# Norms of q taken per head behind its convolution, and exponentials of the broadcast gate rows loaded from DRAM

## The chip, the cores and the metric

The kernel runs on one core of a Trainium2 chip. A core has a matrix engine (TensorE, PE in the profile, with its weight loads as PEld), three engines for element-wise work (VectorE or DVE, ScalarE or ACT, GpSimd or POOL), and SyncE (SP), which here only issues DMAs. Each engine takes its instructions in program order and waits where an operand is not there yet; ACT issues DMAs too, in its own order. The metric is the device time of one execution in microseconds (us), lower is better.

## The reference, cut to what matters

One transformer-like layer works on 1024 latent tokens and 256 context tokens of width 1024. After a modulated norm, one projection feeds two mixers, a gated DeltaNet (four heads of 128, q, k and v through a short convolution) and a rotary retention; then come a gated output projection and a SwiGLU. The change touches the DeltaNet:

```python
y = short_conv(...)                       # 5 taps, then silu; q, k, v per head
q = l2_normalize(q) * (HEAD_DIM ** -0.5)
k = l2_normalize(k)
G = jnp.cumsum(gc, axis=-1)               # running log-decay in a chunk
diff = G[..., :, None] - G[..., None, :]
decay = where(incl, exp(diff), 0)
A = where(strict, (k beta) k^T * decay, 0)
u, w = solve(I + A, [v beta, k beta exp(G)])
qk = (q k^T) * decay
q_dec = q * exp(G)
```

Everything is float32. The kernel takes the norms out of the products: it keeps the sums of squares of q and k and applies them as scales later.

## The kernel before

The token axis is cut into `TT` = 10 tiles of 128 tokens: tiles 0 and 1 are the context, 2 to 9 the latents. There are 4 heads and two directions `d`. A float32 product is made of three passes over high and low parts (`hhi`, `hlo`, `whi`, `wlo`), so most groups of matmuls come as three lines (611 to 613, 371 to 373).

The stages that matter, in the order of the source: the gates (`G`, the cumulative log-decay, is transposed to rows and stored in the DRAM scratch `grow_d`); the convolutions of k (`conv_block(4 + h)`, then `kstat`, which transposes each k tile and takes its squared norm on ACT into `nk`); the convolutions of q (`conv_block(h)`, after which ACT's queue stores the head into the DRAM scratch `qd`, line 682); the two gate groups of the retention, `token_major` 6 and 7 (a `Silu` on ACT at line 532 evacuates their `tm` banks); then the solves. For each token tile `pre(t)` builds what the solve needs; for each of three batches of tiles (`BATCH`) `invert` computes the inverses of 32x32 diagonal blocks in 31 pairs of VectorE instructions (`tmp` at line 765, `X` at 767) and sends them through DRAM (`xd`), and `merge` puts the blocks together with small matmuls. The convolutions of v (`conv_block(8 + h)`, transposes `vT` at line 856, evacuation `vt` on ACT at 859) and the z groups 8 and 9 lie between them as matmul work.

`pre(t)`, lines 701 to 737: load `kc` (line 664); 4 matmuls `kk`; for the latent tiles (t >= 2) load `qc`, transpose it, square it with a row sum into `nq` (lines 710, 712), and 4 matmuls `kq`. Then for each direction: `gw` is loaded from `grow_d`, the same row broadcast to all 128 partitions (256 KB); POOL writes `e` from `gw` with the triangle filled (722); ACT takes 4 exponentials with a bias (726); VectorE multiplies `kk` by `e` into `ut` (730) and `kq` by `e` into `sp` (732); `ut` is stored (733). For t >= 2 ACT also takes the exponential of `gw` itself (735), POOL multiplies it by `qc` (736), and `sp` is stored (737). The pools give two buffers each to `kc`, `qc`, `gw`, `e`, `sp` and `ut`, and three PSUM banks to each of two groups, two to the convolutions.

The order of instructions on each engine is not that of the source: a scheduler with a simulated timeline places them when the program is built, so an edit in one place can move work in another.

Of the kernel before, what the change touches and what calls it, by code (L numbers as in the profile page):

```python
# [8 lines left out]
F32 = mybir.dt.float32  # L9
F32R = mybir.dt.float32r  # L10
I32 = mybir.dt.int32
AF = mybir.ActivationFunctionType
ALU = mybir.AluOpType
# [4 lines left out]
P = 128  # L18
D = 1024
KT = D // P  # L20
NCTX = 256
NLAT = 1024
NTOK = NCTX + NLAT
TT = NTOK // P
LT = NLAT // P
H = 4
# [4 lines left out]
FAR = -1e30  # L31
# [7 lines left out]
def build(nc, tc, ap, dbg=None, stop=None, marks=None):  # L39
    root = ExitStack()  # L40
    V, S, G, T, SY = nc.vector, nc.scalar, nc.gpsimd, nc.tensor, nc.sync
# [17 lines left out]
    def close(p):  # L59
        p_close.pop(id(p)).close()  # L60
# [16 lines left out]
    dr = pool("scratch", space=DRAM)  # L77
# [15 lines left out]
    def bank_b(name):  # L93
        return bank("pb", name)
# [96 lines left out]
    try:  # L191

        cc = const("cc", [P, KT, 2])
        ident = const("ident", [P, P])
# [37 lines left out]
        W2 = None  # L232
# [156 lines left out]
        def token_major(g, tiles, finish, store, pl, q=S):  # L389

            w = [tm_weights(g, kh, pl, q) for kh in range(2)]

            for p in range(0, len(tiles), 2):
                pair = [(t, tm_bank(g)) for t in tiles[p:p + 2]]
                for kh in range(2):
                    for t, o in pair:
                        tm_half(o, w[kh], kh, t)
                for t, o in pair:
                    tm_store(g, t, o, finish, store, pl)
# [47 lines left out]
        W2 = pool("w2", bufs=2)  # L447
# [97 lines left out]
        cw = GS.tile([P, 12, 5], F32, tag="cw", name="cw")  # L545
        SY.dma_start(cw, ap["cw"])
        grow_d = dr.tile([TT * 8, P], F32, tag="grow_d", name="grow_d")


        sd = dr.tile([TT, P, 10, 512], F32, tag="sd", name="sd")  # L550
# [4 lines left out]
        def c8(t, d):  # L555
            return slice(t * 8 + d * 4, t * 8 + d * 4 + 4)
# [39 lines left out]
        gT = AB.tile([80, P], F32, tag="gT", name="gT")  # L596
        V.tensor_copy(gT, ps[:80, :P])
        SY.dma_start(grow_d, gT)
        close(AB)
        CV = pool("cv", side="right")  # L600

# [72 lines left out]
        sv = rsqrt(GS, nkf, TT * H, "sv")  # L674
        V.tensor_tensor(sv, sv, nkf, ALU.mult)
        sv3 = sv.rearrange("p (t h) -> p t h", h=H)
        for h in range(H):
            y = newy()
            conv_block(h, y, True)
            if h < 2:  # L680
                ada_rest(5, h)
            S.dma_start(qd[:, :, h, :].rearrange("t p j -> p t j"),
                        y[:, NCTX:].rearrange("p (t j) -> p t j", j=P))

        checkpoint("q")
        for g in (6, 7):
            token_major(g, LAT, fin_gate, S, W2, SY)
        checkpoint("rg")
        close(R2)
        close(W2)  # L690
# [9 lines left out]
        def pre(t):  # L700
            b, c = where[t]
            kc = load(GP, kd[t], "kc", 2)
            pk = bank_b("kk")
            for h in range(H):
                T.matmul(pk[:, h * P:(h + 1) * P], kc[:, h, :], kc[:, h, :], start=True, stop=True)
            if t >= 2:
                qc = load(GP, qd[t - 2], "qc", 2)
                pn = bank_b("qt")
                for h in range(H):
                    T.transpose(pn[:, h * P:(h + 1) * P], qc[:, h, :], ident)  # L710
                for h in range(H):
                    S.activation(pn[:, h * P:(h + 1) * P], pn[:, h * P:(h + 1) * P], AF.Square, accum_out=nq[:, t - 2, h:h + 1])
                pq = bank_b("kq")
                for h in range(H):
                    T.matmul(pq[:, h * P:(h + 1) * P], kc[:, h, :], qc[:, h, :], start=True, stop=True)
            for d in range(2):
                gw = GP.tile([P, H, P], F32, tag="gw", name="gw", bufs=2)
                SY.dma_start(gw.rearrange("p h i -> p (h i)"),
                             grow_d[c8(t, d), :].rearrange("a b -> (a b)").partition_broadcast(P))
                e = GP.tile([P, H, P], F32, tag="e", name="e", bufs=2)  # L720
                sg = 1 if d == 0 else -1
                G.affine_select(out=e, in_=gw, compare_op=ALU.is_ge, fill=FAR, base=0,
                                pattern=[[0, H], [sg, P]], channel_multiplier=-sg)
                for h in range(H):
                    col = t * 8 + d * 4 + h
                    S.activation(e[:, h, :], e[:, h, :], AF.Exp, bias=sm["nG"][:, col:col + 1])
                if t >= 2:
                    sp = GP.tile([P, 2, H, P], F32, tag="sp", name="sp", bufs=2)
                ut = GU.tile([P, H, P], F32, tag="ut", name="ut", bufs=2)
                V.tensor_tensor(ut.rearrange("p h i -> p (h i)"), pk, e.rearrange("p h i -> p (h i)"), ALU.mult)  # L730
                if t >= 2:
                    V.tensor_tensor(sp[:, 0].rearrange("p h i -> p (h i)"), pq, e.rearrange("p h i -> p (h i)"), ALU.mult)
                SY.dma_start(un[b][:, 1 - d, c * H:(c + 1) * H, :], ut)
                if t >= 2:
                    S.activation(gw, gw, AF.Exp)
                    G.tensor_tensor(sp[:, 1], gw, qc, ALU.mult)
                    SY.dma_start(sd[t, :, 8 - 8 * d:10 - 8 * d], sp.rearrange("p a h i -> p a (h i)"))

# [916 lines left out]
```

## Time and profile before

| | us |
|---|---|
| median of 3 runs | 1479.91 |
| lowest, highest | 1479.66, 1481.7 |
| the profiled execution | 1477.96 |
| its span in the trace | 1476.2 |

The profile covers one execution. Its mean granted TensorE clock is 0.983 of full speed. The gate groups end, and the solves begin, at about 276 us of the span; the first merge's second set of matmuls starts at about 412, and the scans follow from about 480. In rows of the timeline the columns are the start in us, the length in us, engine and line, and the operation with its output and inputs; brackets hold the idle time before it and what ended it. A row of a group ends with its busy time, the mean length of one in ns, and the idle time before its instructions. A row of the waits has the total in us, how often, and the longest. A row of the transfers has their number, KB each and the median time from issue to landing.

### The profile page before, as it was taken

The page shows a single profiled execution, that of the slowest core. Times are in us where ns is not written, and L with a number is a line of the kernel's source. Part 1 is how long each engine was busy: PE and PEld are TensorE (multiplying, and loading weights), DVE is VectorE, ACT ScalarE, POOL GpSimd, SP SyncE. Part 2 cuts the span into 40 slices and gives each one's busy share as a digit, 9 for nine tenths or more (in the row PEclk, how much of TensorE's full clock was granted, in tenths as well). Part 3 has the DMA queues.
Part 4 walks back from the last instruction along what each step waited for, and adds up shares of the span by engine and source line. Part 5 has one row for each costly group of instructions (what it writes and reads, how often), then busy time and mean ns, then how long its engine had stood idle before and what let it go on. Part 6 is the DMA issues. An engine that isn't in the chain of part 4 may idle for free.

```text
span 1476.2 us, 24111 instructions
## 1 busy us (share of the span) xinstructions
PE 1397.2 (95%) x8919; PEld 1199.2 (81%) x8919; DVE 964.6 (65%) x1856; ACT 614.0 (42%) x1326; POOL 590.3 (40%) x501
## 2 busy tenths in 40 slices
PE   7999999986789999899799899999999999999997
PEld 2898888975689999898688688877888888788885
DVE  6566789289792435689676877556555564657477
ACT  5643564587333111245443623233333332444445
POOL 0120010243202344234144688898555552335321
PEclk9999999998899999999899999999999999999999
DMA  9536686688888625996532265674222242776863
GB/s 337 197 105 205 189 249 200 219 264 277 282 216 277 238 76 178 416 341 209 184 125 104 97 238 210 242 264 162 105 97 105 107 151 79 260 260 194 288 216 114
DMA packets 170421, 298.14 MB, mean 202 GB/s; under 512 B 43496, under 2 KB 93880, under 8 KB 165952
## 3 DMA queue, kind: packets, MB, share of 16 engines
q1 hardware_dynamic: 118752, 253.17, 50.2%
q10 hardware_dynamic: 49072, 35.83, 7.8%
q0 software_dynamic: 2480, 7.60, 1.4%
q8 instruction: 70, 1.15, 0.3%
q14 instruction: 47, 0.39, 0.1%
HBM read 206.60 MB, written 89.96 MB: 201 GB/s over the span
## 4 chain that ended last, share of the span: by engine, by line
PE 55%; POOL 6%; DMA 5%; DVE 4%; issue 2%; ACT 2%; SPq 1%; ACTq 0%; POOLq 0%; DVEq 0%
PE ffn L1344 7%; PE ffn L1342 6%; PE ffn L1343 6%; PE fo L1470 4%; PE fo L1469 4%; PE fo L1468 4%; PE tm L371 3%; PE tm L373 3%; PE tm L372 3%; PE op L1203 2%; PE op L1201 2%; PE op L1202 2%; DMA wd<-tw 2%; POOL ws L1315 1%; DMA pk<-sd 1%
## 5 line engine op out<-in xcount | busy, mean ns | idle before, releaser
L371 PE MATMUL tm<-whi,hhi 128*128 128x256 f32 (+1 forms) x704 | 199.5, 287 | 7.7 <-ACT vt L859 3.4
L372 PE MATMUL tm<-wlo,hhi 128*128 128x256 f32 (+1 forms) x704 | 199.3, 285 | 2.4 <-issue 2.0
L373 PE MATMUL tm<-whi,hlo 128*128 128x256 f32 (+1 forms) x704 | 197.7, 285 | 0.0
L371 PEld LDWEIGHTS tm<-whi,hhi 128*128 128x128 f32 x704 | 132.8, 190 | 11.8 <-ACT vt L859 3.6
L1342 PE MATMUL ffn<-t,whi 128*128 128x512 f32 x352 | 136.9, 390 | 1.3 <-ACT whi L344 1.3
L1344 PE MATMUL ffn<-t,wlo 128*128 128x512 f32 x352 | 137.0, 390 | 1.0 <-DVE wlo L345 1.0
L1343 PE MATMUL ffn<-t,whi 128*128 128x512 f32 x352 | 137.0, 389 | 0.0
L372 PEld LDWEIGHTS tm<-wlo,hhi 128*128 128x128 f32 x704 | 133.7, 190 | 2.1 <-issue 0.9
L373 PEld LDWEIGHTS tm<-whi,hlo 128*128 128x128 f32 x704 | 132.8, 190 | 2.6 <-issue 1.8
L344 ACT ACTIVATE whi<-wraw 128x512 fp32r<-128x512 f32 (+2 forms) x98 | 75.1, 771 | 141.4 <-PE ffn L1343 80.5
L344 ACT ACTIVATE whi<-ws 128x512 fp32r<-128x512 f32 x88 | 55.6, 632 | 171.5 <-PE ffn L1343 123.4
L345 DVE TENSOR_TENSOR wlo<-ws,whi 128x512 fp32r<-128x512 f32 x88 | 93.9, 1068 | 47.0 <-ACT whi L344 46.8
L1469 PE MATMUL fo<-wlo,ahi 128*128 128x512 f32 x308 | 120.2, 390 | 2.1 <-DVE wlo L345 2.1
L1468 PE MATMUL fo<-whi,ahi 128*128 128x512 f32 x308 | 119.3, 390 | 0.7 <-ACT ahi L344 0.7
L1470 PE MATMUL fo<-whi,alo 128*128 128x512 f32 x308 | 119.0, 390 | 0.0
L345 DVE TENSOR_TENSOR wlo<-wraw,whi 128x512 fp32r<-128x512 f32 (+2 forms) x92 | 99.4, 1082 | 24.6 <-ACT whi L344 24.6
L1342 PE MATMUL ffn<-b,whi 128*128 128x512 f32 x264 | 103.8, 393 | 4.4 <-ACT whi L344 4.4
L1344 PE MATMUL ffn<-b,wlo 128*128 128x512 f32 x264 | 103.6, 393 | 0.8 <-DVE wlo L345 0.8
L1343 PE MATMUL ffn<-b,whi 128*128 128x512 f32 x264 | 103.4, 392 | 0.0
L612 PE MATMUL b<-hlo,whi 128*128 128x512 f32 (+1 forms) x256 | 94.4, 369 | 0.0
L613 PE MATMUL b<-hhi,wlo 128*128 128x512 f32 (+1 forms) x256 | 94.3, 368 | 0.0
L611 PE MATMUL b<-hhi,whi 128*128 128x512 f32 (+1 forms) x256 | 94.3, 368 | 0.0
(446 smaller groups left out, 3448.1 us busy)
## 6 DMA issues: line engine op xcount, KB each, us to landing
adaw<-ada SPq DMA_DIRECT2D x48, 512.0 KB, 4.4
pk<-sd SPq DMA_DIRECT2D x16, 1536.0 KB, 10.0
wraw<-wfi SPq DMA_DIRECT2D x44, 512.0 KB, 3.7
ar<-ad SPq DMA_DIRECT2D x33, 512.0 KB, 4.7
w<-wfo SPq DMA_DIRECT2D x22, 512.0 KB, 5.7
wd<-tw SPq DMA_DIRECT2D x11, 1024.0 KB, 4.8
ad<-act SPq DMA_DIRECT2D x20, 512.0 KB, 3.0
raw<-wd SPq DMA_DIRECT2D x20, 512.0 KB, 4.9
```

The lines of the kernel that those rows point to most:

```text
L344: S.activation(hi, raw, AF.Copy)
L345: e.tensor_tensor(lo, raw, hi.bitcast(F32), ALU.subtract)
L371: T.matmul(o, hhi[:, k, tsl], whi[:, k % 4, :], start=(k == 0), stop=False)
L372: T.matmul(o, hhi[:, k, tsl], wlo[:, k % 4, :], start=False, stop=False)
L373: T.matmul(o, hlo[:, k, tsl], whi[:, k % 4, :], start=False, stop=(k == KT - 1))
L612: T.matmul(o, whi[:, k, :], hl, start=False, stop=False)
L1342: T.matmul(o, whi[:, k, :], xhi(xn, slice(0, 4), k), start=(first and k == 0), stop=False, **kw)
L1343: T.matmul(o, whi[:, k, :], xlo(xn, slice(0, 4), k), start=False, stop=False, **kw)
L1344: T.matmul(o, wlo[:, k, :], xhi(xn, slice(0, 4), k), start=False, stop=(k == 3), **kw)
L1468: T.matmul(po[g][i], ahi[:, ts], whi, start=(j == 0 and not kw), stop=False, **kw)
L1469: T.matmul(po[g][i], ahi[:, ts], wlo, start=False, stop=False, **kw)
L1470: T.matmul(po[g][i], alo[:, ts], whi, start=False, stop=(j == FH - 1), **kw)
```

## The change

There are two parts. First, the squared norms of q are taken per head from the convolution's own output `y` (a new function `qstat`: eight transposes into two PSUM banks and eight squares with row sums), called for head h - 1 after the convolution of head h, and for the last head between groups 6 and 7. The transposes and squares in `pre(t)` are gone. Second, the exponential of the transposed gates is taken once on ACT (`gE`, 80x128), and stored in a second scratch `grow_e`. In `pre(t)` the log row is now loaded straight into `e` and masked in place, and for t >= 2 the exponential row is loaded into `gw` from `grow_e`, 16 more loads of 256 KB; the 16 exponentials of `gw` are gone.

```diff
--- before.py
+++ after.py
@@ -545,6 +545,7 @@
         cw = GS.tile([P, 12, 5], F32, tag="cw", name="cw")
         SY.dma_start(cw, ap["cw"])
         grow_d = dr.tile([TT * 8, P], F32, tag="grow_d", name="grow_d")
+        grow_e = dr.tile([TT * 8, P], F32, tag="grow_e", name="grow_e")
 
 
         sd = dr.tile([TT, P, 10, 512], F32, tag="sd", name="sd")
@@ -596,6 +597,9 @@
         gT = AB.tile([80, P], F32, tag="gT", name="gT")
         V.tensor_copy(gT, ps[:80, :P])
         SY.dma_start(grow_d, gT)
+        gE = AB.tile([80, P], F32, tag="gE", name="gE")
+        S.activation(gE, ps[:80, :P], AF.Exp)
+        SY.dma_start(grow_e, gE)
         close(AB)
         CV = pool("cv", side="right")
 
@@ -674,6 +678,17 @@
         sv = rsqrt(GS, nkf, TT * H, "sv")
         V.tensor_tensor(sv, sv, nkf, ALU.mult)
         sv3 = sv.rearrange("p (t h) -> p t h", h=H)
+        def qstat(h, y):
+
+            for l0 in (0, 4):
+                pn = bank_b("qt")
+                for i in range(4):
+                    T.transpose(pn[:, i * P:(i + 1) * P], y[:, NCTX + (l0 + i) * P:NCTX + (l0 + i + 1) * P], ident)
+                for i in range(4):
+                    S.activation(pn[:, i * P:(i + 1) * P], pn[:, i * P:(i + 1) * P], AF.Square,
+                                 accum_out=nq[:, l0 + i, h:h + 1])
+
+        qys = []
         for h in range(H):
             y = newy()
             conv_block(h, y, True)
@@ -681,10 +696,14 @@
                 ada_rest(5, h)
             S.dma_start(qd[:, :, h, :].rearrange("t p j -> p t j"),
                         y[:, NCTX:].rearrange("p (t j) -> p t j", j=P))
+            qys.append(y)
+            if h:
+                qstat(h - 1, qys[h - 1])
 
         checkpoint("q")
-        for g in (6, 7):
-            token_major(g, LAT, fin_gate, S, W2, SY)
+        token_major(6, LAT, fin_gate, S, W2, SY)
+        qstat(H - 1, qys[H - 1])
+        token_major(7, LAT, fin_gate, S, W2, SY)
         checkpoint("rg")
         close(R2)
         close(W2)
@@ -705,21 +724,19 @@
                 T.matmul(pk[:, h * P:(h + 1) * P], kc[:, h, :], kc[:, h, :], start=True, stop=True)
             if t >= 2:
                 qc = load(GP, qd[t - 2], "qc", 2)
-                pn = bank_b("qt")
-                for h in range(H):
-                    T.transpose(pn[:, h * P:(h + 1) * P], qc[:, h, :], ident)
-                for h in range(H):
-                    S.activation(pn[:, h * P:(h + 1) * P], pn[:, h * P:(h + 1) * P], AF.Square, accum_out=nq[:, t - 2, h:h + 1])
                 pq = bank_b("kq")
                 for h in range(H):
                     T.matmul(pq[:, h * P:(h + 1) * P], kc[:, h, :], qc[:, h, :], start=True, stop=True)
             for d in range(2):
-                gw = GP.tile([P, H, P], F32, tag="gw", name="gw", bufs=2)
-                SY.dma_start(gw.rearrange("p h i -> p (h i)"),
+                e = GP.tile([P, H, P], F32, tag="e", name="e", bufs=2)
+                SY.dma_start(e.rearrange("p h i -> p (h i)"),
                              grow_d[c8(t, d), :].rearrange("a b -> (a b)").partition_broadcast(P))
-                e = GP.tile([P, H, P], F32, tag="e", name="e", bufs=2)
+                if t >= 2:
+                    gw = GP.tile([P, H, P], F32, tag="gw", name="gw", bufs=2)
+                    SY.dma_start(gw.rearrange("p h i -> p (h i)"),
+                                 grow_e[c8(t, d), :].rearrange("a b -> (a b)").partition_broadcast(P))
                 sg = 1 if d == 0 else -1
-                G.affine_select(out=e, in_=gw, compare_op=ALU.is_ge, fill=FAR, base=0,
+                G.affine_select(out=e, in_=e, compare_op=ALU.is_ge, fill=FAR, base=0,
                                 pattern=[[0, H], [sg, P]], channel_multiplier=-sg)
                 for h in range(H):
                     col = t * 8 + d * 4 + h
@@ -732,7 +749,6 @@
                     V.tensor_tensor(sp[:, 0].rearrange("p h i -> p (h i)"), pq, e.rearrange("p h i -> p (h i)"), ALU.mult)
                 SY.dma_start(un[b][:, 1 - d, c * H:(c + 1) * H, :], ut)
                 if t >= 2:
-                    S.activation(gw, gw, AF.Exp)
                     G.tensor_tensor(sp[:, 1], gw, qc, ALU.mult)
                     SY.dma_start(sd[t, :, 8 - 8 * d:10 - 8 * d], sp.rearrange("p a h i -> p a (h i)"))
```

What this does to the order on the engines is shown at three places. The first is SP's queue where `pre` begins. `kc` and `qc` are the k and q tiles, `gw` and `e` the rows broadcast from `grow_d` and `grow_e`; the numbers tell buffers apart. Before:

```order
L506 DMA grow1_1231<-row_2267 1x512
L664 DMA kc_2895<-sd_1296 128x512
L718 DMA gw_2902<-grow_d_1295 128x512
L718 DMA gw_2915<-grow_d_1295 128x512
L664 DMA kc_2928<-sd_1296 128x512
L664 DMA qc_2968<-qd_1297 128x512
L664 DMA qc_3027<-qd_1297 128x512
L718 DMA gw_2935<-grow_d_1295 128x512
L718 DMA gw_2948<-grow_d_1295 128x512
L664 DMA kc_2961<-sd_1296 128x512
L733 DMA un0_2892<-ut_2912 128x512
```

After:

```order
L506 DMA grow1_1231<-row_2271 1x512
L668 DMA kc_2971<-sd_1297 128x512
L732 DMA e_2978<-grow_d_1295 128x512
L732 DMA e_2990<-grow_d_1295 128x512
L668 DMA kc_3002<-sd_1297 128x512
L736 DMA gw_3049<-grow_e_1296 128x512
L736 DMA gw_3067<-grow_e_1296 128x512
L668 DMA qc_3040<-qd_1298 128x512
L668 DMA qc_3090<-qd_1298 128x512
L736 DMA gw_3099<-grow_e_1296 128x512
L668 DMA kc_3033<-sd_1297 128x512
L750 DMA un0_2968<-ut_2987 128x512
```

A third load from `grow_e`, `gw_3099`, which takes the buffer of `gw_3049`, now stands ahead of the third tile's `kc_3033`; and the rows of the second tile have moved behind it.

The second place is ACT's order around the last q head's `Silu` (`y`) and its store to `qd`; `res` are evacuations of gate tiles, `qt` squares of q. Before:

```order
L532 ACTIVATE res_2642<-tm_2590 128x256
L344 ACTIVATE whi_2651<-wraw_2653 128x1024
L354 DMA wraw_3921<-wg 128x8x128
L387 DMA rd_115<-res_2642 128x256
L614 ACTIVATE u_3544<-b2_3545 128x256
L615 ACTIVATE y_3537<-b2_3545,cw_1293 128x256
L624 ACTIVATE y_2341<-y_2341 128x1024
L532 ACTIVATE res_2707<-tm_2657 128x256
L682 DMA qd_1297<-y_2341 128x8x128
```

After:

```order
L743 ACTIVATE e_2990<-e_2990,nG_1284 128x128 x2
L688 ACTIVATE qt_2449,nq_1292<-qt_2449 128x128
L688 ACTIVATE qt_2372,nq_1292<-qt_2372 128x128
L628 ACT_TABLE_LOAD
L628 ACTIVATE y_2381<-y_2381 128x1024
L688 ACTIVATE qt_2449,nq_1292<-qt_2449 128x128
L688 ACTIVATE qt_2372,nq_1292<-qt_2372 128x128
L688 ACTIVATE qt_2458,nq_1292<-qt_2458 128x128
L532 ACTIVATE res_2895<-tm_2845 128x256
L697 DMA qd_1298<-y_2381 128x8x128
```

The `Silu` and the store stand behind the first exponentials, a table load and more squares, and behind the evacuation of the third pair of gate tiles (`tm_2845`) instead of that of the first (`tm_2657`). The 35 matmuls of the first v convolution that PE had between the gate tiles come after them now, and 24 transposes of q stand there.

The third place is SP's queue ahead of the first merge; `xd0` are the inverses of batch 0, `U0` and `t64` the merge's operands, `U1` those of the next one. Before:

```order
L783 DMA U1_4550<-un1_2893 128x4096
L771 DMA xd0_3079<-X_3086 64x1024 x2
L771 DMA xd0_3079<-XT_3184 64x1024 x2
L751 DMA yr_4440<-un2_2894 16x32x32 x3
L783 DMA U0_4175<-un0_2892 128x4096
L872 DMA rope_4049<-rope 128x1280
L751 DMA yr_4440<-un2_2894 16x32x32
L788 DMA t64_4177<-xd0_3079 32x32x32 x4
L787 DMA U0_4175<-xd0_3079 32x32x32 x4
```

After:

```order
L787 DMA xd0_3133<-X_3140 64x1024 x2
L787 DMA xd0_3133<-XT_3238 64x1024 x2
L750 DMA un2_2970<-ut_4147 128x512
L753 DMA sd_1297<-sp_4146 128x1024
L799 DMA U0_4175<-un0_2968 128x4096
L888 DMA rope_4067<-rope 128x1280
L750 DMA un2_2970<-ut_4165 128x512
L753 DMA sd_1297<-sp_4164 128x1024
L804 DMA t64_4177<-xd0_3133 32x32x32 x4
L803 DMA U0_4175<-xd0_3133 32x32x32 x4
L767 DMA yr_4440<-un2_2970 16x32x32 x4
L799 DMA U1_4550<-un1_2969 128x4096
```

The 2 MB load of `U1` and the `yr` loads have moved behind the operands of the first merge, and stores of the last tile's `ut` and `sp` stand ahead of these. On PE 48 more matmuls of group 8 stand ahead of the merge.

## The prediction

> **What bounds the kernel now.** I read the page's busy times first, then TensorE's waits by line, then a cut into windows at the places where those waits fall, then engine groups, transfers and the timeline inside the stretch that remains.
>
> ```profile
> PE 1397.2 (95%) x8919; PEld 1199.2 (81%) x8919; DVE 964.6 (65%) x1856; ACT 614.0 (42%) x1326; POOL 590.3 (40%) x501
> 276.00:312.00 36.00, 34.90 (x214) 30.09 (x214) 20.16 (x26) 27.68 (x76) 14.69 (x18) 1.00 0.81 256
> 312.00:373.00 61.00, 42.80 (x252) 36.79 (x250) 57.59 (x84) 50.09 (x147) 26.68 (x22) 0.90 0.85 270
> 373.00:412.00 39.00, 31.18 (x383) 30.10 (x389) 31.68 (x78) 10.98 (x24) 5.78 (x5) 0.93 0.94 278
> 412.00:480.00 68.00, 62.60 (x1333) 59.82 (x1324) 38.60 (x106) 21.01 (x39) 8.76 (x18) 0.97 0.84 248
> 480.00:580.00 100.00, 100.00 (x855) 99.85 (x855) 42.25 (x130) 10.92 (x14) 43.47 (x86) 1.00 0.43 157
> ```
>
> The first row is the whole span. The others are windows: length, then busy time of PE, PEld, DVE, ACT and POOL, then granted clock and DMA share. TensorE (PE) is the bound: 95% busy, and 100.00 of 100.00 us from 480 on. Its idle time in the solve stages is 1.1 + 18.2 + 7.8 + 5.4 = 32.5 us. The changed order gives PE the same matmuls, and the same order again soon after the merges. So I count one thing: what happens to those 32.5 us, plus any new stall earlier. (The clock is 0.90 in the stretch with most idle time; what it costs I leave in the range.)
>
> ```profile
> PE vT L856 <- ACT y L624: 9.6, 2, 9.3
> PE kk L705 <- issue: 8.4, 3, 6.7
> PE tm L371 <- ACT vt L859: 3.4, 1, 3.4
> PE tm L371 <- ACT whi L344: 1.4, 1, 1.4
> PE m L814 <- DMA U<-xd: 0.9, 1, 0.9
> POOL e L722 <- DMA gw<-grow_d: 28.1, 10, 6.3
> ACT e L726 <- POOL e L722: 11.7, 9, 2.6
> ```
>
> PE's waits between 276 and 480 name ScalarE (ACT) and a hole ahead of `kk`, but POOL waits for loads and ACT for POOL. The loop is a ring with two buffers; no one engine sets it alone. In 312 to 373 VectorE (DVE) has 57.59 of 61 us busy against ACT's 50.09: it is the fuller one.
>
> **What leaves ACT.**
>
> ```profile
> L735 ACT ACTIVATE gw<-gw 128x512 f32<-128x512 f32 x16 | 9.9, 617 | 0.0
> L712 ACT ACTIVATE qt<-qt 128x128 f32<-128x128 f32 x32 | 8.7, 271 | 1.1 <-ACT qt L712 0.8
> 288.60 0.26 ACT L712 ACTIVATE qt<-qt 128x128 f32<-128x128 f32 x1
> 289.01 0.26 ACT L712 ACTIVATE qt<-qt 128x128 f32<-128x128 f32 x1
> L726 ACT ACT_TABLE_LOAD x4 | 5.1, 1283 | 0.4 <-ACT res L532 0.4
> ```
>
> Squares start 0.41 us apart (288.60, 289.01), so 32 of them are about 13 us; they move into the group 6/7 stage, where PE is full. The 16 `Exp`s of `gw` are 9.9 us busy, some 8.3 net of the overlap with the next instruction, and they go for good. So 21 us of ACT leaves the solve stage. Against that ACT gets eight more table loads in its order (28 for 20), 8 × 1.283 = 10.3 us, six of them late, where `Exp`s of the last batch stand between z's `Silu`s.
>
> The Trainium skill, "ScalarE: Activation LUTs", section "What ACT_TABLE_LOAD costs", gives about 1283 ns for a load and about 1380 ns more for a drain, 2.66 us a switch, which speaks against this change. The load agrees with the row above; no drain follows it in this trace:
>
> ```profile
> 277.79 1.28 ACT L726 ACT_TABLE_LOAD   x1 [0.39 <-ACT res L532]
> 279.09 2.45 ACT L726 ACTIVATE e<-e,nG 128x128 f32<-128x128 f32 x8
> ```
>
> The `Exp` starts 1.30 us after its load. By the page the eight would be an estimated 21.3 us, and nothing would leave ACT on balance.
>
> The new exponential `gE` (one of 80x128) and its store of 40 KB stand in the gating stage, long before; I charge nothing, covered by the k convolutions' matmuls behind them, and at most one load and one short activation, 1.7 us, if that cover is gone. The `affine_select` in place costs what it cost.
>
> **Term A: the start, a stall of about 7 us.** ACT's and SP's orders at the head of the stage matter here (the places shown with the change).
>
> ```profile
> 258.26 0.38 ACTq L682 DMA_DIRECT2D qd<-y  x1
> 272.30 0.38 ACT L532 ACTIVATE res<-tm 128x256 f32<-128x256 f32 x1
> 276.17 0.28 PE L373 MATMUL tm<-whi,hlo 128*128 128x256 f32 x1
> 276.29 1.95 PE L705 MATMUL kk<-kc 128*128 128x128 f32 x16
> 283.18 0.39 PE L611 MATMUL b<-hhi,whi 128*128 128x512 f32 x1
> 283.40 0.39 PE L612 MATMUL b<-hlo,whi 128*128 128x512 f32 x1
> 283.64 0.61 PE L705 MATMUL kk<-kc 128*128 128x128 f32 x4
> qd<-y ACTq DMA_DIRECT2D x4, 512.0 KB, 4.2
> qc<-qd SPq DMA_DIRECT2D x6, 256.0 KB, 5.5
> kc<-sd SPq DMA_DIRECT2D x8, 256.0 KB, 3.7
> gw<-grow_d SPq DMA_DIRECT2D x16, 256.0 KB, 4.9
> 287.08 1.30 POOL L736 TENSOR_TENSOR sp<-gw,qc 128x512 f32<-128x512 f32 x1 [0.91 <-ACT gw L735]
> ```
>
> The store of the last q head left at 258.26. In the changed order it stands behind `res_2895`, the evacuation of the third pair of gate tiles; its counterpart ran at 272.30. Ahead of that pair 35 v-convolution matmuls are gone (24 of 256 columns at 0.12 us, as from 276.17 to 276.29, and 11 of 512 at 0.22, as from 283.18 to 283.40: 5.3 us), and 24 transposes have come (2.9 us, at 0.12 us each as in the 16 `kk` of 276.29). With some 2 us of stall, since squares and two table loads stand ahead of evacuations, the store leaves near 272. Then 4.2 to land, 5.5 for `qc`, 1.3 for POOL's product with the exponential row, about 0.8 of issue, and 3.7 for the third tile's `kc`: SP's next load of `gw` waits for the buffer that this product frees, and `kc_3033` is queued behind it. That is 287.5. PE comes to this `kk` at 276.3 - 5.3 + 3.9 (32 transposes) + 2 + 2 + 4 (24 v-convolution matmuls at 0.12, six at 0.22) = 282.9. So PE stalls 5 us there, plus the 2. Bounds: nothing, if the buffers are free in time, and 11, if landings take the 6.3 that POOL's longest wait for a row shows.
>
> This stall is no term by itself. PE does the same work up to the last transposes of v, so what counts is when these can start, and VectorE decides that.
>
> **Term B: the last transposes of v, +4.5 us.**
>
> ```profile
> 370.34 1.27 DVE L621 SCALAR_TENSOR_TENSOR y<-u,cw,y 128x1022 f32<-128x1022 f32 x1
> 373.51 0.68 DVE L730 TENSOR_TENSOR ut<-kk,e 128x512 f32<-128x512 f32 x1
> 375.11 0.37 DVE L765 TENSOR_TENSOR tmp<-L,X 128x207 f32<-128x207 f32 x1
> 375.93 0.36 DVE L765 TENSOR_TENSOR tmp<-L,X 128x192 f32<-128x192 f32 x1
> 375.06 2.39 PE L856 MATMUL vT<-ident,y 128*128 128x128 f32 x10 [9.27 <-ACT y L624]
> ```
>
> The last tap (370.34) releases the `Silu` and then the transposes (375.06). The first v head's taps start some 9 us later than before: the 5.3 us of its matmuls that left the gate stage, and most of A. I add 2 because `e` is now itself the load's target: both its buffers stay taken until VectorE's two products have read them, so the next load starts later. Lag 11. In the changed order VectorE has three `ut`, two `sp` (0.68 each by the row of `ut`) and three steps of the inversion (0.82 each, 375.11 to 375.93) fewer ahead of the last tap: 5.9 us. Of its 3.4 idle us in 312 to 373 I let it use 1.6. The tap ends 11 - 5.9 - 1.6 = 3.5 later, the transposes start at 378.6, and about 1 us of `kq` that stood ahead of them is left for after: +4.5. Bounds: -5 (no lag), +8 (no idle used, `e` 2 us later still).
>
> **Term C: to the first merge, -3.5.**
>
> ```profile
> 391.78 0.56 SPq L783 DMA_DIRECT2D U<-un  x1
> 393.59 10.27 SPq L788 DMA_DIRECT2D t<-xd  x4
> 411.85 0.22 PE L814 MATMUL m<-U,xt 32*32 32x32 f32 x2 [0.93 <-DMA U<-xd]
> ```
>
> From 375.06 to 411.85 PE waits 3.4 us for ACT's `vt`, 1.4 for `whi`, 0.9 for `U`: 5.7 in all, the most that can be had. In the changed order 48 more matmuls of group 8 (5.6 us) stand ahead of the merge, and one of the two 2 MB loads of `U` stands behind the loads that the merge needs, not ahead of them as in 391.78, 393.59. That covers the last two waits (2.3); of the first, which hangs on v's stores, I take a third. Nothing more, because the loads of `t` now also stand behind SP's stores of the last tile's `ut` and `sp`, and so behind the lag. Bounds: 0 and -5.7.
>
> **Term D: given back, +1.5.** The 5.6 us of matmuls used as cover here are missing in 412 to 480, where PE already idles 5.4. Between none and all of it; I take a quarter, since VectorE and ACT have only 38.6 and 21.0 of 68 us there.
>
> **Sum.** 4.5 - 3.5 + 1.5 = +2.5 us. The profiled execution took 1477.96 us (its span 1476.2); the median of the three runs is 1479.91, 1.95 more. 1477.96 + 2.5 + 1.95 = 1482.4, so **1482**: ACT's 21 us leave, and PE was not waiting for them. The 16 added loads of 256 KB (4.2 MB) I charge nothing of their own, with a DMA share of 0.81 to 0.85 as cover; without it they are 16 us of transfers at 256 to 270 GB/s.
>
> **Rivals.** *Slower, by the ring of `e` and the fuller queues.* A load, an `affine_select`, four `Exp`s and two products per buffer: if landings go from 4.9 to POOL's longest 6.3, each of the eight turns of two buffers costs 1.4 more, 11 us in all, of which VectorE's 3.4 idle us hide some. +8 on the forecast, 1490. It decides from a start of the last transposes later than 379.1, where the forecast passes 1482.9. For it: POOL's 28.1 us of such waits, and share 0.85. *Faster, by cover.* The lag is taken up by VectorE's shorter queue and the earlier `Exp`s: the transposes start at 373 instead of 378.6 and all of C is had, 1482.4 - 5.6 - 2.2 = 1474.6. It decides where they start before 373.2, or before 375.4 with all of C. For it: 5.9 us less in the fullest engine's queue. *Larger gain.* ACT was the pacer: the 9.6 and 8.4 us of waits for `vT` and `kk` go by three quarters, 1466; ACT's 50.09 of 61 speaks against it. *Table loads.* The six late ones hold z's evacuations by 7.7 us, PE's three banks hide half: 1486.
>
> The page named above would double the price of the table loads; the trace so far doesn't.
>
> **How the numbers follow.** Forecast 0.42, ring 0.25, cover 0.20, larger gain 0.08, table loads 0.05. A change of 0.2% (3 us) is about what a measurement of this kernel can tell from none. Faster than 1477.0: 0.20 + 0.08 and a little of the forecast, 0.30. Within: 0.25, most of the forecast. Slower than 1482.9: 0.25, 0.05 and 0.15 of the forecast, whose own range is 1477 to 1487: 0.45. The whole range leaves out the largest gain and the worst of the ring: 1470 to 1491.
>
> **What would show it.** Right: the store of the last q head leaves near 272, PE waits some 5 us ahead of the third tile's `kk`, the last block of `vT` starts at 378 to 379, ACT's `gw` row is gone and its busy time in 312 to 373 falls below 40 with PE's idle time there no smaller. Wrong: `kk` of the third tile unstalled (A), `vT` before 375 (ACT or the shorter queue did count), `vT` after 380 (ring), or group 8 waiting for ACT behind table loads in 412 to 480.

## The result and the profile after

| | before | after |
|---|---|---|
| median, us | 1480.16 (4 runs) | 1491.44 (4 runs) |
| lowest, highest | 1479.66, 1481.7 | 1490.46, 1492.49 |
| span of the profiled execution | 1476.2 | 1490.6 |

The changed kernel is slower: 1.0075 times the time of before (95% interval 1.0057 to 1.0092), 11 us by the medians and 14.4 by the spans of the two profiled executions. These two lie on opposite sides of their medians (1477.96 below the 1479.91 of the first three runs, 1492.49 above 1491.44), so some 3 of the 14.4 us are spread between runs. The forecast was 1482 us; the time lies 0.4 us above the upper end of the range. The rival "slower, by the ring of `e`" was put at 1490.

The same cuts of the span as before. The columns are length, busy time of PE, PEld, DVE, ACT and POOL, granted clock, DMA share and GB/s; the first line is the page's, over the whole span.

```profile
PE 1404.8 (94%) x8919; PEld 1208.5 (81%) x8919; DVE 970.6 (65%) x1856; ACT 615.2 (41%) x1319; POOL 595.0 (40%) x501
240.00:276.00 36.00, 32.69 (x246) 29.99 (x244) 19.77 (x35) 20.95 (x72) 4.11 (x3) 1.00 0.50 156
276.00:312.00 36.00, 34.14 (x211) 30.08 (x211) 15.69 (x21) 18.36 (x58) 11.67 (x13) 1.00 0.70 216
312.00:373.00 61.00, 45.89 (x260) 39.79 (x259) 51.83 (x76) 39.62 (x90) 25.59 (x20) 0.90 0.92 292
373.00:412.00 39.00, 29.04 (x222) 28.34 (x221) 29.15 (x62) 22.37 (x42) 10.87 (x10) 0.85 0.98 305
412.00:480.00 68.00, 59.85 (x1164) 56.94 (x1165) 50.17 (x128) 18.25 (x33) 9.27 (x14) 0.85 0.75 197
480.00:580.00 100.00, 98.65 (x1036) 97.53 (x1036) 41.71 (x125) 15.52 (x25) 37.32 (x72) 0.98 0.62 223
```

Read PE's column and the clock beside it. ACT lost what it was to lose (39.62 us busy instead of 50.09 in 312 to 373), and PE's idle time there did fall, from 18.2 to 15.1 us. But 3.3 us appeared ahead of 276, and 373 to 580 has 19.5 us of idle (10.0 + 8.2 + 1.4) where there were 13.2. The clock fell from 0.93 and 0.97 to 0.85 in 373 to 480. Over the whole span the same 8919 matmuls keep PE busy for 7.6 us more (1404.8 against 1397.2), and it idles for 6.8 us more (85.8 against 79.0). So in this pair of executions about half of the loss is idle time, and half is matmuls run at a lower clock.

PE's waits between 276 and 480, with the total, the number and the longest:

```profile
PE kq L729 <- issue: 14.1, 4, 9.9
PE tm L371 <- ACT whi L344: 7.3, 1, 7.3
PE m L830 <- issue: 7.2, 2, 5.0
PE vT L872 <- ACT y L628: 4.2, 2, 2.8
```

The wait for `vT` has shrunk (9.6 before); waits for `kq`, for weights and in the merge have grown. The timeline shows where these come from (start, length, engine or its DMA queue; brackets: idle time before it):

```profile
273.42 0.38 ACTq L697 DMA_DIRECT2D qd<-y  x1
286.39 1.13 PE L724 MATMUL kk<-kc 128*128 128x128 f32 x8 [1.23 <-DMA kc<-sd]
280.21 1.29 DVE L747 TENSOR_TENSOR ut<-kk,e 128x512 f32<-128x512 f32 x2 [14.20 <-PE kk L724]
398.31 0.68 DVE L747 TENSOR_TENSOR ut<-kk,e 128x512 f32<-128x512 f32 x1
378.30 2.40 PE L872 MATMUL vT<-ident,y 128*128 128x128 f32 x10 [2.78 <-ACT y L628]
391.74 1.12 DVE L785 COPY XT<-X 128x1024 f32<-128x1024 f32 x1
400.72 12.42 SPq L804 DMA_DIRECT2D t<-xd  x4
410.79 0.33 ACTq L387 DMA_DIRECT2D zd<-res  x1
411.17 2.00 ACT L344 ACTIVATE whi<-wraw 128x1024 fp32r<-128x1024 f32 x2 [9.83 <-DMA rope<-rope]
412.27 0.58 PE L371 MATMUL tm<-whi,hhi 128*128 128x256 f32 x1 [7.35 <-ACT whi L344]
421.62 1.44 PE L823 MATMUL m<-t,U 32*32 32x32 f32 x128
426.02 0.21 PE L830 MATMUL m<-U,xt 32*32 32x32 f32 x1
```

The first and the last of the 20 `ut` products are 118.1 us apart (280.2 to 398.3); before it was 96.0, from 277.48 to 373.51:

```profile
277.48 1.29 DVE L730 TENSOR_TENSOR ut<-kk,e 128x512 f32<-128x512 f32 x2 [15.70 <-POOL X L755]
```

The inverse of batch 0 is done at 391.7 (before: 381.0), the loads of `t<-xd` go out at 400.7 (393.6), and the first merge starts at 421.6, 17.4 us later than before (404.2), and its second set of matmuls at 426.0, where it was 410.7. In the kernel before:

```profile
404.21 0.58 PE L807 MATMUL m<-t,U 32*32 32x32 f32 x4
410.66 0.21 PE L814 MATMUL m<-U,xt 32*32 32x32 f32 x1
```

The last transposes of v are only 3.2 us late.

### The profile page after: what moved, and what is told of

Read it like the earlier page. It is cut to its first block, busy times and chain, and to the rows that moved or that the text cites. A ratio compares the mean times of both kernels' runs of the same rounds, so it can differ in the third digit from the quotient of the medians.

```text
span 1490.6 us, 24157 instructions
## 1 busy us (share of the span) xinstructions
PE 1404.8 (94%) x8919; PEld 1208.5 (81%) x8919; DVE 970.6 (65%) x1856; ACT 615.2 (41%) x1319; POOL 595.0 (40%) x501
## 4 chain that ended last, share of the span: by engine, by line
PE 56%; DMA 8%; POOL 6%; DVE 6%; issue 4%; ACT 3%; SPq 0%; ACTq 0%; POOLq 0%; DVEq 0%
PE ffn L1360 6%; PE ffn L1358 6%; PE ffn L1359 6%; PE fo L1484 4%; PE fo L1486 4%; PE fo L1485 4%; PE tm L371 3%; PE tm L372 3%; PE tm L373 3%; PE op L1217 2%; PE op L1219 2%; PE op L1218 2%; DMA wd<-tw 2%; POOL ws L1331 1%; DMA e<-grow_d 1%
## 5 line engine op out<-in xcount | busy, mean ns | idle before, releaser
L372 PE MATMUL tm<-wlo,hhi 128*128 128x256 f32 (+1 forms) x704 | 202.4, 290 | 2.6 <-DVE wlo L345 2.6
L371 PEld LDWEIGHTS tm<-whi,hhi 128*128 128x128 f32 x704 | 135.2, 194 | 15.3 <-ACT whi L344 7.5
```

The costliest lines, as they stand in the source:

```text
L371: T.matmul(o, hhi[:, k, tsl], whi[:, k % 4, :], start=(k == 0), stop=False)
L372: T.matmul(o, hhi[:, k, tsl], wlo[:, k % 4, :], start=False, stop=False)
```

## The experiments

Each was compared with runs of the kernel before on the same chip. The table gives the ratio to these with its interval, and three times from each profile: the first and last `ut` with their distance, the end of batch 0's inverse (the start of its 31st step), and the issue of the first `t<-xd`. Within about 3 us of one another medians of this table are not told apart; some variants spread by 9 to 12 us from run to run (q_y2: 1486.1 to 1495.2, z_copy: 1485.8 to 1497.5). A profile shows one execution, which can lie at the edge of that: q_y2's took 1486.1 us, before_ur's 1499.4.

| run | median us | ratio (95%) | 20 `ut`, us | inverse | t<-xd |
|---|---|---|---|---|---|
| before | 1480.16 | | 277.5 to 373.5: 96.0 | 380.8 | 393.6 |
| after | 1491.44 | 1.0075 (1.0057, 1.0092) | 280.2 to 398.3: 118.1 | 391.5 | 400.7 |
| q_only | 1491.90 | 1.0081 (1.0057, 1.0106) | 282.9 to 379.4: 96.5 | 386.9 | 399.2 |
| rows_only | 1486.76 | 1.0055 (1.0036, 1.0073) | 280.2 to 396.0: 115.8 | 384.4 | 394.4 |
| no_gw | 1500.92 | 1.0141 (1.0115, 1.0168) | 282.6 to 393.3: 110.7 | 395.8 | 411.7 |
| z_copy | 1492.25 | 1.0086 (1.0062, 1.0110) | 279.7 to 399.1: 119.4 | 392.3 | 401.7 |
| q_kd | 1487.72 | 1.0051 (1.0033, 1.0069) | 284.0 to 381.8: 97.8 | 389.3 | 400.7 |
| after_kd | 1493.43 | 1.0091 (1.0068, 1.0113) | 280.1 to 397.9: 117.8 | 391.1 | 401.2 |
| no_gw_e4 | 1489.73 | 1.0063 (1.0044, 1.0081) | 289.8 to 376.4: 86.6 | 387.9 | 397.8 |
| e3gw1 | 1501.96 | 1.0138 (1.0123, 1.0153) | 287.4 to 392.1: 104.7 | 395.2 | 405.7 |
| q_y2 | 1493.96 | 1.0095 (1.0070, 1.0121) | 281.2 to 378.9: 97.8 | 385.9 | 409.8 |
| q_pa | 1499.91 | 1.0139 (1.0113, 1.0165) | 275.1 to 393.8: 118.7 | 398.3 | 416.4 |
| after_y2 | 1493.25 | 1.0104 (1.0084, 1.0124) | 283.4 to 400.7: 117.3 | 389.4 | 399.5 |
| no_gw_e4_y2 | 1481.45 | 1.0023 (1.0010, 1.0036) | 282.3 to 366.6: 84.3 | 379.9 | 401.8 |
| q_y2_rope | 1492.55 | 1.0092 (1.0057, 1.0128) | 283.1 to 381.6: 98.5 | 388.5 | 414.3 |
| before_rope | 1478.25 | 0.9996 (0.9975, 1.0017) | 277.5 to 374.8: 97.2 | 382.0 | 394.1 |
| after_y2_rope | 1490.64 | 1.0083 (1.0055, 1.0110) | 283.9 to 401.2: 117.3 | 389.5 | 399.3 |
| q_y2_ur | 1488.99 | 1.0073 (1.0050, 1.0097) | 281.2 to 380.1: 98.9 | 387.0 | 411.2 |
| before_ur | 1491.81 | 1.0082 (1.0066, 1.0098) | 277.7 to 376.0: 98.2 | 383.3 | 402.8 |
| after_y2_ur | 1504.07 | 1.0169 (1.0148, 1.0190) | 282.2 to 401.7: 119.4 | 388.6 | 407.5 |

**The two parts alone, the volume, and the table loads.** q_only keeps `qstat` and leaves the rows as they were:

```diff
-                e = GP.tile([P, H, P], F32, tag="e", name="e", bufs=2)
-                SY.dma_start(e..., grow_d[...])
-                if t >= 2:
-                    gw = GP.tile(...); SY.dma_start(gw..., grow_e[...])
-                G.affine_select(out=e, in_=e, ...)
+                gw = GP.tile([P, H, P], F32, tag="gw", name="gw", bufs=2)
+                SY.dma_start(gw..., grow_d[...])
+                e = GP.tile([P, H, P], F32, tag="e", name="e", bufs=2)
+                G.affine_select(out=e, in_=gw, ...)
...
+                    S.activation(gw, gw, AF.Exp)
```

> Only the first part of the change: q's norms per head behind the convolution; the rows are loaded and exponentiated as before. Two theories. R (the rows: e as load target, 16 more loads, SP's order behind them): this part costs nothing much, 1478 to 1482 us, and the first merge's operands are loaded at the time of before (t<-xd issued within 3 us of 393.6). S (the start: the squares ahead of the last q head's store delay the first latent tile, and the lag goes through): 1486 to 1491, with PE waiting some 5 us ahead of the third tile's kk and the last transposes of v 3 us or more late.

rows_only is the kernel before with the opposite of this edit (and `gE`, `grow_e`):

> Only the second part: e loaded directly, exponential rows from the second scratch; q's transposes and squares stay in the pre loop. R: the whole loss, 1488 to 1493, with the loads of t<-xd issued 5 us or more later than in the kernel before and PE idle ahead of the first merge. S: 1478 to 1483, as the store of the last q head leaves as early as before.

no_gw is the changed kernel with

```diff
-                if t >= 2:
-                    gw = GP.tile(...); SY.dma_start(gw..., grow_e[...])
...
-                    G.tensor_tensor(sp[:, 1], gw, qc, ALU.mult)
+                    G.tensor_tensor(sp[:, 1], qc, qc, ALU.mult)
```

> The changed kernel without the 16 added loads: the product that used the exponential row multiplies q by itself, so the factor exp(G) of q is left out. If the volume of these loads (4.2 MB) or their places in SP's order make the loss: 1479 to 1484. If it is e as load target (its two buffers held until VectorE's products): no better than 1488. If S: 1487 to 1491.

z_copy replaces `fin_gate` by `fin_copy` for groups 8 and 9:

> The changed kernel with the gate groups 8 and 9 evacuated by a plain copy, so z's silu is left out and the six late table loads go (22 instead of 28); the order on every engine is otherwise the same. If the table loads hold z's evacuations and the last exponentials: 1483 to 1487. If they are hidden (R): within 2 us of the changed kernel, 1489 to 1492.

Neither theory held as it stood: each part alone is slower than before, by 12 and by some 8 us, and together they cost 11, not 20. The distance of the `ut` products tells the parts apart. It is 96.5 us with the first part, as before, and 115.8 with the second; without the 16 loads it is still 110.7. So the loop is stretched by `e` as the target of the load, and only a third of the stretch goes with the added loads or their places in SP's order. The length of the loop does not decide the time alone: no_gw is the slowest of the four, with a shorter loop, and its `t<-xd` is issued at 411.7. Why its end is so late was not taken apart. Table loads are no cause: six fewer of them, with the order otherwise kept, change nothing that can be measured. (The Trainium skill, "ScalarE: Activation LUTs", section "What ACT_TABLE_LOAD costs", prices a switch at 2.66 us, so an estimated 16 us of ACT for six; by this run, none of it reaches the end.)

**The start, and the ring of `e`.** q_kd and after_kd take away the wait for the store of the last q head, in q_only and in the changed kernel:

```diff
-                qc = load(GP, qd[t - 2], "qc", 2)
+                qc = load(GP, kd[t], "qc", 2)
```

> Only the first part of the change (as in q_only), but pre loads its q tiles from the scratch of k, so the store of the last q head is waited for by nobody; the products with q are then products with k. The orders of the engines stay those of q_only but for a place or two. S (the late store delays the first latent tile and the lag goes through): the first ut of a latent tile comes some 6 us earlier than in q_only, and the time falls from 1491.9 to 1479 to 1485. R, in its form for this part (the matmuls' order, or the squares in the gate stage, cost it): 1489 to 1492.

> The changed kernel with the same exchange: q tiles loaded from the scratch of k, so no wait for the last q head. If the start is the cause: 1479 to 1485. If the ring of e is (the 20 ut multiplies take 118 us instead of 96 in the changed kernel, with either start): the 20 ut still take 112 us or more, and the time falls by 4 us at most, 1487 to 1491.

no_gw_e4 is no_gw with `bufs=4` for `e`; e3gw1 is the changed kernel with 3 buffers for `e` and 1 for `gw`:

> As no_gw (the factor exp(G) of q left out, no loads for it), with four buffers for e instead of two. Ring theory: the 20 ut multiplies take 96 us or less instead of the 111 of no_gw, and the time falls from 1500.9 to below 1488. If VectorE or the transfers set the pace: still 105 us or more, 1495 to 1502.

> The changed kernel with three buffers for e and one for the exponential rows. Ring of e: the 20 ut multiplies take 100 to 110 us instead of 118, time 1480 to 1488. If e's buffers are not what the loop waits for: 118 us or more, and 1491 or slower.

The ring stands: with four buffers the products take 86.6 us instead of 110.7 (they start 7 us later and end 17 earlier), and the time falls by 11 us, to 1489.7, which is 1.7 above what was expected. With three the distance is 104.7, as expected, but the time is no better (1502): with one buffer for `gw` its loads stand behind one another (POOL waits 27.2 us for them between 276 and 420, 1.9 in the changed kernel), and the merge comes later still. The late store of q, on which term A rested, is not the cause: after_kd is no faster (1493), and q_kd is some 4 us faster (1.0051 against 1.0081, with intervals that overlap), which is neither what S nor what R had said. Its `ut` products begin no earlier (284.0 against 282.9), nor does the fifth of them, the first of a latent tile (293.8 against 292.7). This part of S falls.

**What the moved transposes hold.** A q head's `y` is freed by its last reader. That was the store to `qd`; now it is `qstat`'s transposes, which take their PSUM banks from the group that the solve uses, and which the order puts into the gate stage. `y` has three buffers, and the first v head takes one of them. This is what pushed 35 matmuls of the first v convolution out of the gate stage. q_y2 gives q heads 2 and 3 buffers of their own (the main lines; the offset `yo` is handed on in `conv_block` and `qstat`):

```diff
-            y = newy()
-            conv_block(h, y, True)
+            own = h >= 2
+            yo = NCTX if own else 0
+            y = R2.tile([P, NLAT], F32, tag="yq", name="yq", bufs=2) if own else newy()
+            conv_block(h, y, True, yo)
```

> Only the first part of the change (as q_only), with the convolution outputs of q heads 2 and 3 in two buffers of their own, so that the first v head no longer waits for the transposes of a q head to release its buffer. In the order the first v convolution is back in the gate stage (35 of its matmuls ahead of the first kk), and the last q head's store stands where it stood before. Buffer theory (y held by the moved transposes pushed the v convolution back, and VectorE starved): 1474 to 1482, first v transposes within 5 us of 305 us (q_only: 325). Rival (moving the squares and transposes into the gate stage costs by itself): 1487 to 1492.

q_pa lets the transposes of q_only go early instead (`bank_a("qt")` for `bank_b("qt")`); after_y2 is the whole change with q_y2's edit; no_gw_e4_y2 adds that edit to no_gw_e4:

> Only the first part, with qstat's transposes in the PSUM banks of the token-major groups instead of those of the solve. In the order they run in the q convolution stage then, 24 of 32 ahead of the gate groups, and y is released early. Buffer theory: 1474 to 1484, unless the banks taken from the gate groups stall these (PE idle between 200 and 276 would show it). Rival as for q_y2: 1487 or more.

> The whole change with the two buffers of q_y2. If the loss has two causes, y's buffers at the start and the ring of e in the loop: the start is mended, the 20 ut multiplies still take 112 us or more, and the time is that of rows_only, 1484 to 1489. If y's buffers were all: 1475 to 1482. If they were nothing: 1490 to 1493.

> The whole change with both causes mended as far as the memory allows it: two own buffers for q heads 2 and 3, four buffers for e, and no exponential rows at all (the factor exp(G) of q is left out, q is multiplied by itself). If the two causes explain the loss, and ScalarE's relief is worth something: 1466 to 1476, below the kernel before. If ScalarE's relief is worth nothing: 1477 to 1482. If a third cause is missing: above 1484.

The start was mended as far as it was meant to be. The first transposes of v in q_only and in q_y2 (305.0 in the kernel before):

```profile
324.87 1.26 PE L866 MATMUL vT<-ident,y 128*128 128x128 f32 x10
```

```profile
310.07 1.31 PE L868 MATMUL vT<-ident,y 128*128 128x128 f32 x10 [1.62 <-ACT y L624]
```

The last tap of the v convolutions, too, came back from 380.9 to 372.7 (370.3 before). So `y`'s buffers did hold the v convolutions. But the time of q_y2 did not fall, which the buffer theory had said. q_pa tells nothing here: the gate groups end 17.5 us later in it (293.7 against 276.2), and POOL, which has written two `e` by 260.6, waits 33.5 us for them ahead of the third. after_y2 keeps the stretched loop (117.3) and the time. With both mended, no_gw_e4_y2 is back to 1.0023 of before, 8 to 10 us below the changed kernel. The net loss left there is some 3 us, although ScalarE's relief is there in full (no exponentials of `gw`, no squares in the loop). That the relief is worth nothing, and that no third cause is left, is not shown by it: the order of its end is another one (`t<-xd` at 401.8 against 393.6, though the inverse is done 0.9 us earlier), so a loss there could hide a gain.

**What replaced the start in q_y2.** SP's queue in q_y2, ahead of the merge:

```profile
381.30 1.57 SPq L795 DMA_DIRECT2D U<-un  x2
398.40 0.33 SPq L884 DMA_DIRECT2D rope<-rope  x1
398.78 0.51 SPq L783 DMA_DIRECT2D xd<-X  x1
...
409.81 3.18 SPq L800 DMA_DIRECT2D t<-xd  x4
```

The inverse is done at 385.9, but SP stops for 15.5 us (382.9 to 398.4) and stores it at 398.8. The waits of SP's queue between 370 and 425 name what ended the stop ahead of `rope`, the landing of stores of v tiles:

```profile
SPq L884 <- DMA sd<-vt: 15.4, 2, 14.7
```

I first took `rope` for the cause, whose load stands there. q_y2_rope, before_rope and after_y2_rope issue it from POOL (`G.dma_start(rope, ap["rope"])`):

> As q_y2 (first part of the change, two own buffers for q heads 2 and 3), with the load of rope issued by POOL instead of SP, where it stopped the queue for 15 us ahead of the store of batch 0's inverse. If that place was the rest of the loss: xd stored at 385 to 390 instead of 398.8, time 1474 to 1483. If moving the squares costs by itself: 1487 or more.

> Control: the kernel before with only the load of rope issued by POOL. There it stood for less than a microsecond behind the loads of yr and U, so: within 3 us of the kernel before, 1476 to 1483.

> The whole change with the two own buffers for q and rope's load on POOL's queue. What is left is the ring of e: the 20 ut multiplies take 112 us or more, time 1484 to 1490. If the queue's order was the cause of that too: 1483 or less.

That was wrong: 1492.5, and SP stops all the same, now between two of the stores:

```profile
383.93 1.65 SPq L795 DMA_DIRECT2D U<-un  x2
388.74 0.51 SPq L783 DMA_DIRECT2D xd<-X  x1
392.81 0.48 SPq L783 DMA_DIRECT2D xd<-XT  x1
393.35 0.59 SPq L783 DMA_DIRECT2D xd<-X  x1
403.12 0.45 SPq L783 DMA_DIRECT2D xd<-XT  x1
```

What both have ahead of the store is the two loads of `U`, 2 MB each; in the kernel before, one stands ahead and one behind. But no_gw_e4_y2 has both ahead as well:

```profile
372.76 1.28 SPq L797 DMA_DIRECT2D U<-un  x2
389.98 0.33 SPq L886 DMA_DIRECT2D rope<-rope  x1
```

SP stops there for 15.9 us, an inverse that is done at 379.9 is stored at 390.4, and the time is within some 3 us of before all the same. So such a stop does not make a loss of 12 us by itself. The last three runs issue the two loads of `U` from POOL as well (`G.dma_start(uu..., un[b])`):

> As q_y2_rope (first part of the change, two own buffers for q heads 2 and 3, rope's load on POOL's queue), with the 2 MB loads of U issued by POOL too. If these loads ahead of the store of the inverse were the rest of the loss: xd stored within 386 to 392 without a stop, 1472 to 1483. If moving the squares costs by itself: 1487 or more.

> Control: the kernel before with the loads of rope and of U issued by POOL. Its order had one of the two loads of U ahead of the store of the inverse and one behind. Within 4 us of the kernel before, 1474 to 1482.

> The whole change with the two own buffers and the same two loads on POOL's queue. The ring of e is left: the 20 ut multiplies take 112 us or more, and the time lies 5 us or more above that of q_y2_ur. If the ring costs nothing once SP is free: within 3 us of q_y2_ur.

In q_y2_ur the inverse is stored without a stop (387.3 to 391.7), as expected; the stop moved to the next loads (`yr`, 11.79 us from 392.5), and the time stayed at 1489. The control told more than the test: with both `U` loads out by 383, ahead of the store of the inverse, the kernel before is itself 12 us slower. Its products and its last tap (372.8) come some 2.5 us later. SP's queue stops in the store of the inverse, and PE waits 11.3 us for ACT's `vt`, where it waited 3.4:

```profile
383.47 1.16 SPq L771 DMA_DIRECT2D xd<-X  x2
385.98 10.67 SPq L771 DMA_DIRECT2D xd<-XT  x2
400.01 2.63 SPq L751 DMA_DIRECT2D yr<-un  x4
PE tm L371 <- ACT vt L859: 11.3, 1, 11.3
396.27 1.14 ACT L859 ACTIVATE vt<-vT,svy 128x128 f32<-128x128 f32 x4 [15.74 <-DMA sd<-vt]
```

In the kernel before:

```profile
383.24 4.87 SPq L771 DMA_DIRECT2D xd<-XT  x2
385.83 1.14 ACT L859 ACTIVATE vt<-vT,svy 128x128 f32<-128x128 f32 x4 [7.78 <-DMA sd<-vt]
```

There `yr` was at 389.3. So moving these 4 MB of loads, to another queue and the second of them from 391.8 to 382.7, is worth some 12 us by itself (before_rope shows that `rope` is not it). In the profile the longest part is on PE's own path: ACT's last evacuations of v wait 8 us longer for v's stores to land, and PE waits 7.9 us longer for them. That the loads hold these stores up, because they run at the same time, is argued and not tested. Against its own control q_y2_ur lies 2.8 us lower, and the whole change (after_y2_ur) 12.3 us higher: with the transposes' buffers mended and these queues, the first part costs nothing that can be told, and the second part, with the ring of `e`, costs 12 us or, against q_y2_ur, 15.

No run beat the kernel before: before_rope cannot be told from it (0.9975 to 1.0017).

## Why the prediction was wrong

*What bounds it.* Right as far as the runs go: no kernel with ScalarE's relief beat the kernel before, and taking six late table loads out (z_copy) gained nothing. Wrong in one thing: the clock was left in the range, and it carries about half of the loss in the two profiled executions. (How much of that belongs to the change is open: in no_gw_e4_y2, within some 3 us of before, PE is busy for 1402.5 us too.) In the changed kernel PE idles from 405 to 412.3, and the windows behind it show what follows:

```profile
405.00:412.30 7.30, 0.03 (x1) 0.03 (x1) 0.04 (x1) 1.13 (x2) 0.00 (x0) 0.75 0.99 318
414.00:416.00 2.00, 2.00 (x11) 2.00 (x11) 1.97 (x4) 0.00 (x0) 0.56 (x1) 0.50 1.13 197
416.00:418.00 2.00, 2.00 (x12) 2.00 (x11) 1.83 (x6) 0.39 (x1) 0.00 (x0) 0.50 0.90 217
418.00:420.00 2.00, 2.00 (x15) 2.00 (x15) 1.86 (x5) 0.39 (x1) 0.00 (x0) 0.79 1.19 185
```

PE is busy throughout 414 to 418 at half its clock. (The Trainium skill, "TensorE: Matmul & The Clock Gate", section "Part 1: The HAM clock gate", states half clock after at least one idle window of about 3.4 us, and full clock after at least one busy window as long. The trace agrees: the half clock lasts to between 418 and 420, some 6 us after the work resumed at 412.3.)

*Term A.* The mechanism was there, and the sizes were mixed: the store of q left at 273.4 (forecast 272), the third tile's `kk` ran at 286.4 (287.5), but PE reached it later than I had counted and waited 1.2 us, not 5. And it was not what mattered: after_kd, without the wait for the store, is no faster. What I took for its consequence, the late v convolution, has another cause that I had seen in the order (35 matmuls moved) and not explained: the release of `y`.

*Term B.* The time of the last transposes came out as forecast, 378.3 against 378.6. But the lag put on the ring of `e` was mis-sized: I added 2 us, and the loop took 22 us more (118.1 against 96.0). VectorE's taps did not wait for it, which is why the transposes were nearly on time; the last tiles' products did, and the inverse with them.

*Term C* is the step that failed: -3.5 forecast. By the place where the merge waits (`m` on line 830, 426.0 against 410.7 for line 814), PE is 15.3 us late with 49 more matmuls of group 9 done, 5.8 us at 0.118 each: 9.5 us worse. Of that 4.3 were there at the transposes (3.2, and 1.1 for eight `kq` matmuls left over), so C was +5.2. I had let the merge's operands follow the transposes. They follow the inverse, whose first `X` came at 335.1 instead of 314.4 and whose last was 10.7 us late, and then the last tile's products, whose stores stand ahead of `t<-xd` on SP (the order that I had quoted). The 48 matmuls meant as cover did not cover. I had put them down to group 8, but all 192 matmuls of group 8 are done ahead of the first merge in both kernels; what was added is of group 9 (72 of its matmuls in the trace ahead of `m` on line 830, 23 ahead of line 814 before). Group 9 needs new weights, so its first matmul waits 7.3 us for `whi`. ACT reaches that at 411.2, behind a store of a gate tile that is ready at 401.3 and goes out at 410.8; the profile names the landing of `rope`'s load, which SP had issued at 397.9, as what ended this wait.

*Term D*: +1.5 forecast, +4.9 by the difference (14.4 - 9.5), the lower clock included.

*The rivals.* "Slower, by the ring of `e`" had the right sign, place and near enough the time (1490), with 0.25; its stated price, 11 us on landings, was not the mechanism. The loads of `grow_d` do not land so much later (5.2 us in the median against 4.9; the added ones from `grow_e` take 6.3); the buffer is free later, since VectorE reads it last. By its own test (last transposes after 379.1) the trace would have ruled it out. *Table loads* falls by z_copy.

*What stays open.* The loss of the first part alone, 12 us, is not settled. The release of `y` is shown to move the v convolutions, and the place of 4 MB of loads is shown to be worth 12 us in the kernel before; but no run with that part and the rows of before came below 1487 as a median, so that these two make the 12 us is argued, not shown, and no_gw_e4_y2, with both loads ahead of the store and no such loss, speaks against the second. Why a store of ACT waits for the landing of `rope`'s load, which it does not use, was not tried, nor was the changed kernel with that load alone moved.

## What to carry to other kernels

Moving work off an engine that nobody waits for gains nothing, and what the moved or merged instructions hold is the price: before an edit makes a later instruction the last reader of a buffer, follow who takes that buffer next. In place is not free: a load target that is also the result stays taken until its last consumer has read it, which here turned 96 us of loop into 118. A chain through DRAM follows the queue's order: ask what stands ahead of its stores. And matmuls are cover only if their own operands are there: ask which engine has to make their weights, and what that engine is waiting for.

## What the runs showed that I had not expected

Behind two loads of 2 MB, SP's queue stood still for 15.5 us in q_y2 (382.9 to 398.4) and for 15.9 in no_gw_e4_y2 (374.0 to 390.0), and the profile names the landing of stores of v tiles, not the loads, as the end of it. Issuing these loads from POOL instead, the second of them 9 us earlier, made the kernel before 12 us slower. ACT's store that was ready at 401.3 went out at 410.8, when `rope`'s load had landed; in the kernel before one waited from 398.5 to 403.8, and there the profile names the landing of a load of `yr`. Neither load is an operand of the store: by the profile, a transfer here waited for one with which it shares no data.
